# Log-softmax over rows of 50000: dealing a tile's stretches to the partitions in 16 groups of 8

## The chip, the cores and the metric

The kernel runs on one core of one Trainium2 chip. The time is the device time of that core in microseconds (us), the median of several executions. The kernel before takes 7589.62 us (three runs, 7589.4 to 7590.59).

## What is computed

```python
x: (16, 512, 50000) float32, normally distributed

max_x = np.max(x, axis=-1, keepdims=True)
shifted = x - max_x
log_sum_exp = np.log(np.sum(np.exp(shifted), axis=-1, keepdims=True))
return (shifted - log_sum_exp).astype(np.float32)
```

There are 16 x 512 = 8192 rows of 50000 numbers. Input and output are 1638.4 MB each. Every row needs its maximum and the sum of its exponentials before its first output can be written.

## The kernel before

A row is cut into G = 4 parts of 12500 numbers, which is 50000 bytes, and each part lies in one partition. A tile is 32 rows: 128 partitions with one stretch of 50000 bytes each, 6250 KB (of 1024 bytes), and there are 256 tiles. Before the change, partition p of tile t holds stretch p of the tile, so that the four parts of a row are in four neighbouring partitions.

```python
P = 128
SQ = 32          # the transpose works on squares of 32
G = 4            # parts of a row
R = P // G       # rows of a tile
C = 3125         # a piece of a part; NS = 4 pieces
NBUF = 4         # tile buffers
...
xt = xf.rearrange("(t r) (g w) -> t (r g) w", r=R, g=G)
ot = of.rearrange("(t r) (g w) -> t (r g) w", r=R, g=G)

def run(a, first, n):
    part = a[first : first + NBUF * n].rearrange("(q i) p w -> q i p w", i=NBUF)
    return lambda q, i: part[bass.ds(q, 1), i].rearrange("o p w -> (o p) w")
```

The engines run side by side and are joined by semaphores. SyncE issues the loads, one for a tile. The first four are issued at once; each later one waits until the store has emptied its buffer:

```python
def load(j, src):
    sync.dma_start(out=bufs[j], in_=src).then_inc(landed[j], 16)

for t in range(NBUF):
    load(t, xt[t])
src = run(xt, NBUF, rounds)
with sync.Fori(0, rounds) as q:
    for j in range(NBUF):
        take(sync, stored[j])
        load(j, src(q, j))
```

VectorE takes the maximum of each piece (line 197), then the smallest negated maximum of the partition (line 202). In `share` it makes the four partitions of a row agree: a transpose of 32 x 32 squares (line 165), a reduction over the parts of a row (line 168), a copy that gives the result back to each part (line 174), and a transpose back (line 180). It later scales the sums (line 208) and subtracts maximum and logarithm in place (line 185):

```python
vector.transpose(out=allneg, in_=negp.to_broadcast([P, SQ]))
vector.tensor_reduce(
    out=rowneg, in_=allneg.rearrange("p (r g) -> p r g", g=G), op=ALU.min, axis=AX)
vector.tensor_copy(
    out=spread.rearrange("p (r g) -> p r g", g=G),
    in_=rowneg[:, :, None].to_broadcast([P, SQ // G, G]))
vector.transpose(out=negmaxs[k], in_=spread)
...
vector.tensor_scalar(
    out=buf, in0=buf, scalar1=negmaxs[k][:, 0:1], scalar2=logs[k],
    op0=ALU.add, op1=ALU.subtract)
```

(The semaphores are cut from this excerpt.) ScalarE takes the exponentials of each piece and their sum (line 239), and issues the stores. The store of a tile is issued in the middle of the next tile's exponentials; the last tile's goes out in four pieces:

```python
for c in range(NS):
    if c == GATE and dst is not None:
        store((j - 1) % NBUF, dst, bufs[(j - 1) % NBUF])
    ... exponential of piece c of tile j ...
...
for c in range(NS):
    store(NBUF - 1, ot[ntiles - 1][:, cols(c)], bufs[NBUF - 1][:, cols(c)])
```

TensorE adds the sums of a row's parts by a product with a matrix `ones` (line 277), which has a one wherever two partitions hold parts of the same row. GpSimd builds that matrix once, at the start, with a fill and two selections.

Of the kernel before, what the change touches and what calls it, by code (L numbers as in the profile page):

```python
# [10 lines left out]
ALU = mybir.AluOpType  # L11
AX = mybir.AxisListType.X

P = 128
SQ = 32

G = 4
R = P // G
C = 3125
NBUF = 4  # L20

NS = 4

# [21 lines left out]
def take(engine, sem, n=16):  # L45

    engine.wait_ge(sem, n).then_inc(sem, -n)  # L47


def cols(c):  # L50
    return slice(c * C, (c + 1) * C)
# [3 lines left out]
def kernel(  # L55
# [6 lines left out]
    xf = x.flatten_outer_dims()  # L62
    of = out.flatten_outer_dims()
# [3 lines left out]
    ntiles = N // R  # L67


    rounds = (ntiles - NBUF) // NBUF  # L70
    assert ntiles % NBUF == 0 and rounds >= 2

    xt = xf.rearrange("(t r) (g w) -> t (r g) w", r=R, g=G)
    ot = of.rearrange("(t r) (g w) -> t (r g) w", r=R, g=G)

    def run(a, first, n):

        part = a[first : first + NBUF * n].rearrange("(q i) p w -> q i p w", i=NBUF)
        return lambda q, i: part[bass.ds(q, 1), i].rearrange("o p w -> (o p) w")

    data = ctx.enter_context(tc.tile_pool(name="data", bufs=1))
    stats = ctx.enter_context(tc.tile_pool(name="stats", bufs=1))
# [9 lines left out]
    ones = consts.tile([P, P], FP32, name="ones")  # L92
    bufs = [data.tile([P, W], FP32, name=f"buf{j}") for j in range(NBUF)]
    dump = dump_pool.tile([P, C], FP32, name="dump")
    sums = sum_pool.tile([P, NBUF], FP32, name="sums")
    rowsums = [sums[:, k : k + 1] for k in range(NBUF)]

# [15 lines left out]
    def sem(name):  # L113
        return ctx.enter_context(nc.semaphore(name))
# [3 lines left out]
    ready = sem("ones_ready")  # L118
# [11 lines left out]

    @block.gpsimd
    def _(gpsimd):
        view = ones.rearrange("p (r g) -> p r g", g=G)
        gpsimd.memset(ones, 1.0).then_inc(ready)  # L134
        gpsimd.affine_select(  # L135
            out=view, in_=view, pattern=[[-G, R], [0, G]], base=0,
            channel_multiplier=1, compare_op=ALU.is_ge, fill=0.0,
        ).wait_op(ready, 1, "sem-ge").then_inc(ready)
        gpsimd.affine_select(  # L139
            out=view, in_=view, pattern=[[G, R], [0, G]], base=G - 1,  # L140
            channel_multiplier=-1, compare_op=ALU.is_ge, fill=0.0,
        ).wait_op(ready, 2, "sem-ge").then_inc(ready)

    @block.sync
    def _(sync):
# [10 lines that stand above are left out]
        for j in range(NBUF - 1):  # L156
            take(sync, stored[j])
        take(sync, stored[NBUF - 1], 16 * NS)

    @block.vector  # L160
    def _(vector):
        def share(k):

            on_dve.next(
                vector.transpose(out=allneg, in_=negp.to_broadcast([P, SQ]))  # L165
            ).then_inc(on_dve.sem)
            on_dve.next(
                vector.tensor_reduce(  # L168
                    out=rowneg, in_=allneg.rearrange("p (r g) -> p r g", g=G),
                    op=ALU.min, axis=AX,  # L170
                )
            ).then_inc(on_dve.sem)
            on_dve.next(
                vector.tensor_copy(  # L174
                    out=spread.rearrange("p (r g) -> p r g", g=G),
                    in_=rowneg[:, :, None].to_broadcast([P, SQ // G, G]),
                )
            ).then_inc(on_dve.sem)
            on_dve.next(
                vector.transpose(out=negmaxs[k], in_=spread)  # L180
            ).then_inc(agreed.sem)

        def subtract(k, *bufs):
            for n, buf in enumerate(bufs):
                ins = vector.tensor_scalar(  # L185
                    out=buf, in0=buf, scalar1=negmaxs[k][:, 0:1], scalar2=logs[k],
                    op0=ALU.add, op1=ALU.subtract,
                )
                if n == 0:
                    logged.next(ins)  # L190
                ins.then_inc(subtracted.sem)

        def whole(j, by_pieces=False):
            take(vector, landed[j])

            for c in range(NS):
                vector.tensor_reduce(  # L197
                    out=negms[j][:, c : c + 1], in_=bufs[j][:, cols(c)],
                    op=ALU.max, axis=AX, negate=True,
                ).then_inc(shifted.sem if c < NS - 1 else on_dve.sem)  # L200
            on_dve.next(vector.nop()).then_inc(shifted.sem)  # L201
            vector.tensor_reduce(  # L202
                out=negp, in_=negms[j], op=ALU.min, axis=AX
            ).then_inc(on_dve.sem)
            share(j)

            rescaled.next(
                vector.tensor_mul(out=scaleds[j], in0=scales[j], in1=parts[j])  # L208
            ).then_inc(summed.sem)
            subtract(j, *([bufs[j][:, cols(c)] for c in range(NS)] if by_pieces else [bufs[j]]))  # L210

        def settle():
            for count in (on_dve, rescaled, logged):
                count.settle(vector)

        with vector.Fori(0, rounds):
            for j in range(NBUF):
                whole(j)
            settle()
        for j in range(NBUF):  # L220
            whole(j, by_pieces=j == NBUF - 1)

    @block.scalar
    def _(scalar):
        def log(k):
            added.next(
                scalar.activation(out=logs[k], in_=rowsums[k], func=ACT.Ln)  # L227
            ).then_inc(logged.sem)

        def store(j, dst, buf):  # L230
            subtracted.next(scalar.dma_start(out=dst, in_=buf)).then_inc(stored[j], 16)

        def whole(j, dst=None):
# [4 lines that stand above are left out]
                shifted.next(  # L238
                    scalar.activation(  # L239
                        out=dump, in_=bufs[j][:, cols(c)], func=ACT.Exp,  # L240
                        bias=negms[j][:, c : c + 1], scale=1.0,
                        accum_out=parts[j][:, c : c + 1],
                    )
                ).then_inc(on_act.sem)
                on_act.next(scalar.nop())  # L245
            agreed.next(
                scalar.activation(  # L247
                    out=scales[j], in_=negms[j], func=ACT.Exp,
                    bias=negmaxs[j][:, 0:1], scale=-1.0,
                )  # L250
            ).then_inc(rescaled.sem)
            log(j)

        def settle():
            for count in (on_act, shifted, agreed, added, subtracted):
                count.settle(scalar)

        nc.scalar.preload_act_table_set("natural_log_exp_and_others")  # L258
        whole(0)
        settle()  # L260
        dst = run(ot, 0, rounds)
        with scalar.Fori(0, rounds) as q:
            for i in range(NBUF):
                whole((i + 1) % NBUF, dst(q, i))
            settle()
        for t in range(ntiles - NBUF + 1, ntiles - 1):
            whole(t % NBUF, ot[t - 1])
        store(t % NBUF, ot[t], bufs[t % NBUF])
        whole(NBUF - 1)
        for c in range(NS):  # L270
            store(NBUF - 1, ot[ntiles - 1][:, cols(c)], bufs[NBUF - 1][:, cols(c)])

    @block.tensor
    def _(tensor):
        def whole(j):
            for c in range(NS):
                ins = tensor.matmul(  # L277
                    rowsums[j], ones, scaleds[j][:, c : c + 1],
                    start=c == 0, stop=c == NS - 1,
                )  # L280
                if c == 0:
                    summed.next(ins)
            ins.then_inc(added.sem)

        tensor.wait_ge(ready, 3)
        with tensor.Fori(0, rounds):
            for j in range(NBUF):
                whole(j)
            summed.settle(tensor)
        for j in range(NBUF):  # L290
            whole(j)
# [30 lines left out]
```

## Time and profile before

| what | before |
|---|---|
| time, median of 3 | 7589.62 us |
| span of the profiled execution | 7588.4 us |
| VectorE busy | 5440.6 us |
| ScalarE busy | 3184.7 us |
| TensorE busy | 477.9 us |
| bytes moved | 3276.85 MB, mean 432 GB/s |
| a load, from its issue to its landing (median) | 36.7 us |
| a store, likewise | 41.6 us |

A busy time is the time in which an engine had an instruction at work; beside the span it tells how much room the engine has. The transfers run on 16 DMA engines, which loads and stores share; their share of busy time and the GB/s are given for slices of the span. The page also gives, for each queue, the packets and the share of the time of the 16 DMA engines that they took. The trace keeps every packet's start, duration, size and queue, but not the DMA engine that moved it. In the waits, a row names the engine and line that waited, what it waited for, the sum, the number of times and the longest.

### The profile page before, as it was taken

The page shows a single profiled execution, that of the slowest core. Times are in us where ns is not written, and L with a number is a line of the kernel's source. Part 1 is how long each engine was busy: PE and PEld are TensorE (multiplying, and loading weights), DVE is VectorE, ACT ScalarE, POOL GpSimd, SP SyncE. Part 2 cuts the span into 40 slices and gives each one's busy share as a digit, 9 for nine tenths or more (in the row PEclk, how much of TensorE's full clock was granted, in tenths as well). Part 3 has the DMA queues.
Part 4 walks back from the last instruction along what each step waited for, and adds up shares of the span by engine and source line. Part 5 has one row for each costly group of instructions (what it writes and reads, how often), then busy time and mean ns, then how long its engine had stood idle before and what let it go on. Part 6 is the DMA issues. An engine that isn't in the chain of part 4 may idle for free. (4 is left out here: it accounts for less than half of the span.)

```text
span 7588.4 us, 13821 instructions
## 1 busy us (share of the span) xinstructions
PE 477.9 (6%) x2048; PEld 456.0 (6%) x2048; DVE 5440.6 (72%) x2819; ACT 3184.7 (42%) x2561; POOL 1.4 (0%) x7
## 2 busy tenths in 40 slices
PE   0000000000000000000000000000000000000000
PEld 0000000000000000000000000000000000000000
DVE  7767677777777777777777777777777777777776
ACT  4434444344443434444344443434444344444433
POOL 0000000000000000000000000000000000000000
DMA  9999999999999999999999999999999999999999
GB/s 417 432 432 433 434 431 434 434 433 433 434 433 431 434 434 433 431 434 433 432 434 434 431 434 434 432 433 434 434 431 434 434 434 432 434 434 431 434 434 400
DMA packets 74162, 3276.85 MB, mean 432 GB/s; under 512 B 8240, under 2 KB 8240, under 8 KB 8240
## 3 DMA queue, kind: packets, MB, share of 16 engines
q1 hardware_dynamic: 36864, 1638.42, 50.0%
q10 hardware_dynamic: 37296, 1638.42, 50.0%
q14 instruction: 2, 0.02, 0.0%
HBM read 1638.40 MB, written 1638.40 MB: 432 GB/s over the span
## 5 line engine op out<-in xcount | busy, mean ns | idle before, releaser
L239 ACT ACTIVATE dump<-buf,negm 128x3125 f32<-128x3125 f32 x1024 | 2937.3, 2868 | 3805.0 <-DVE negm L197 3765.7
L197 DVE TENSOR_REDUCE negm<-buf 128x1 f32<-128x3125 f32 x1024 | 3418.2, 3400 | 923.3 <-DVEq L47 923.3
L185 DVE TENSOR_SCALAR buf<-buf,negmax,logsum 128x12500 f32<-128x12500 f32 (+1 forms) x259 | 1738.9, 6715 | 553.8 <-ACT logsum L227 553.8
L277 PE MATMUL sums<-scaled,ones 128*128 128x1 f32 x2048 | 477.9, 355 | 7087.2 <-DVE scaled L208 7087.2
L277 PEld LDWEIGHTS sums<-scaled,ones 128*128 128x128 f32 x2048 | 456.0, 328 | 7109.0 <-DVE scaled L208 7109.0
L208 DVE TENSOR_TENSOR scaled<-scale,part 128x4 f32<-128x4 f32 x256 | 41.6, 163 | 580.4 <-ACT scale L247 580.4
L227 ACT ACTIVATE logsum<-sums 128x1 f32<-128x1 f32 x256 | 43.8, 171 | 551.0 <-PE sums L277 551.0
L239 ACT ACTIVATION_READ_ACCUMULATOR dump<-buf,negm 128x1 f32 x1024 | 190.8, 186 | 0.0
L247 ACT ACTIVATE scale<-negm,negmax 128x4 f32<-128x4 f32 x256 | 76.1, 297 | 23.6
L202 DVE TENSOR_REDUCE negp<-negm 128x1 f32<-128x4 f32 x256 | 40.1, 157 | 39.2 <-DVE negm L197 39.2
L180 DVE STREAM_TRANSPOSE negmax<-spread 128x32 f32<-128x32 f32 x256 | 54.2, 212 | 8.9
L165 DVE STREAM_TRANSPOSE allneg<-negp 128x32 f32<-128x32 f32 x256 | 54.1, 211 | 8.9
L168 DVE TENSOR_REDUCE rowneg<-allneg 128x8 f32<-128x32 f32 x256 | 47.6, 186 | 8.9
L174 DVE COPY spread<-rowneg 128x32 f32<-128x32 f32 x256 | 46.3, 181 | 8.9
L258 ACT ACT_TABLE_LOAD x1 | 1.3, 1283 | 1.0 <-SPq L111 1.0
L135 POOL TENSOR_SCALAR_AFFINE_SELECT ones<-ones 128x128 f32<-128x128 f32 x1 | 0.5, 519 | 0.1
L139 POOL TENSOR_SCALAR_AFFINE_SELECT ones<-ones 128x128 f32<-128x128 f32 x1 | 0.5, 519 | 0.1
L134 POOL MEMSET ones<- 128x128 f32 x1 | 0.2, 205 | 0.5 <-SPq L111 0.5
L306 POOL MEMSET const-bfloat16-1.0<- 128x1 bf16 x1 | 0.1, 103 | 0.0
L306 POOL MEMSET const-uint8-127<- 128x1 uint8 x1 | 0.1, 102 | 0.0
L306 POOL MEMSET const-float32-0.0<- 128x1 f32 x1 | 0.1, 99 | 0.3 <-issue 0.3
L306 POOL MEMSET const-float32-1.0<- 128x1 f32 x1 | 0.1, 99 | 0.0
## 6 DMA issues: line engine op xcount, KB each, us to landing
buf<-in_x_dram SPq DMA_DIRECT2D x256, 6250.0 KB, 36.7
out_dram<-buf ACTq DMA_DIRECT2D x255, 6250.0 KB, 41.6
out_dram<-buf ACTq DMA_DIRECT2D x4, 1562.5 KB, 11.3
```

The lines of the kernel that those rows point to most:

```text
L165: vector.transpose(out=allneg, in_=negp.to_broadcast([P, SQ]))
L168: vector.tensor_reduce(out=rowneg, in_=allneg.rearrange("p (r g) -> p r g", g=G), op=ALU.min, axis=AX,)
L174: vector.tensor_copy(out=spread.rearrange("p (r g) -> p r g", g=G), in_=rowneg[:, :, None].to_broadcast([P, SQ // G, G]),)
L180: vector.transpose(out=negmaxs[k], in_=spread)
L185: ins = vector.tensor_scalar(out=buf, in0=buf, scalar1=negmaxs[k][:, 0:1], scalar2=logs[k], op0=ALU.add, op1=ALU.subtract,)
L197: vector.tensor_reduce(out=negms[j][:, c : c + 1], in_=bufs[j][:, cols(c)], op=ALU.max, axis=AX, negate=True,).then_inc(shifted.sem if c < ...
L202: vector.tensor_reduce(out=negp, in_=negms[j], op=ALU.min, axis=AX).then_inc(on_dve.sem)
L208: vector.tensor_mul(out=scaleds[j], in0=scales[j], in1=parts[j])
L227: scalar.activation(out=logs[k], in_=rowsums[k], func=ACT.Ln)
L239: scalar.activation(out=dump, in_=bufs[j][:, cols(c)], func=ACT.Exp, bias=negms[j][:, c : c + 1], scale=1.0, accum_out=parts[j][:, c : c + 1],
L247: scalar.activation(out=scales[j], in_=negms[j], func=ACT.Exp, bias=negmaxs[j][:, 0:1], scale=-1.0,)
L277: ins = tensor.matmul(rowsums[j], ones, scaleds[j][:, c : c + 1], start=c == 0, stop=c == NS - 1,)
```

## The change

The stretches of a tile are dealt to the partitions in another order. Partition p = 8a + b, with a from 0 to 15 and b from 0 to 7, now holds stretch 16b + a of the tile, where before it held stretch p. Sixteen stretches that follow one another in DRAM thus lie in partitions 0, 8, 16, ... 120; the next sixteen lie in partitions 1, 9, 17, and so on. The four parts of a row are 8 partitions apart, and still in one square of 32. [...]

What follows from the new order: the views of a row's parts in `share` step by 8 elements, the matrix `ones` has its ones elsewhere and is built with a fill and four selections, and the last tile's cut stores index one dimension more.

```diff
+STEP = 8
...
-    xt = xf.rearrange("(t r) (g w) -> t (r g) w", r=R, g=G)
-    ot = of.rearrange("(t r) (g w) -> t (r g) w", r=R, g=G)
+    def chunks(a):
+        rows = a.rearrange("n (g w) -> (n g) w", g=G)
+        return rows.rearrange("(t b a) w -> t a b w", a=P // STEP, b=STEP)
+
+    xt, ot = chunks(xf), chunks(of)
...
-        part = a[first : first + NBUF * n].rearrange("(q i) p w -> q i p w", i=NBUF)
-        return lambda q, i: part[bass.ds(q, 1), i].rearrange("o p w -> (o p) w")
+        part = a[first : first + NBUF * n].rearrange("(q i) a b w -> q i a b w", i=NBUF)
+        return lambda q, i: part[bass.ds(q, 1), i].rearrange("o a b w -> (o a) b w")
...
-        gpsimd.memset(ones, 1.0).then_inc(ready)
-        (two selections)
+        view = ones.rearrange("p (b g r) -> p b g r", g=G, r=STEP)
+        gpsimd.memset(ones, 0.0).then_inc(ready)
+        for i in range(G):
+            gpsimd.affine_select(
+                out=view, in_=view, pattern=[[-SQ, P // SQ], [0, G], [-1, STEP]],
+                base=-STEP * i, channel_multiplier=1,
+                compare_op=ALU.not_equal, fill=1.0,
+            ).wait_op(ready, i + 1, "sem-ge").then_inc(ready)
...
-                    out=rowneg, in_=allneg.rearrange("p (r g) -> p r g", g=G),
+                    out=rowneg, in_=allneg.rearrange("p (g r) -> p r g", g=G),
...
-                    out=spread.rearrange("p (r g) -> p r g", g=G),
+                    out=spread.rearrange("p (g r) -> p r g", g=G),
...
-            store(NBUF - 1, ot[ntiles - 1][:, cols(c)], bufs[NBUF - 1][:, cols(c)])
+            store(NBUF - 1, ot[ntiles - 1][:, :, cols(c)], bufs[NBUF - 1][:, cols(c)])
...
-        tensor.wait_ge(ready, 3)
+        tensor.wait_ge(ready, G + 1)
```

More of the change, by code (lines that the diff above doesn't have):

```diff
@@ L132, in _ @@
     def _(gpsimd):
-        view = ones.rearrange("p (r g) -> p r g", g=G)
-        gpsimd.memset(ones, 1.0).then_inc(ready)
[L135 to L142, printed above, removed]
+        view = ones.rearrange("p (b g r) -> p b g r", g=G, r=STEP)
[6 more added lines that the diff above has]
+            ).wait_op(ready, i + 1, "sem-ge").then_inc(ready)
     @block.sync
```

## The prediction

> **What bounds the kernel now.** I read the summary page first (busy shares, then the transfer rows), then the chain that ended last, then the waits, then the table by stage. The first page lines say nearly all of it:
>
> ```profile
> span 7588.4 us, 13821 instructions
> PE 477.9 (6%) x2048; PEld 456.0 (6%) x2048; DVE 5440.6 (72%) x2819; ACT 3184.7 (42%) x2561; POOL 1.4 (0%) x7
> ...
> DMA  9999999999999999999999999999999999999999
> ...
> DMA packets 74162, 3276.85 MB, mean 432 GB/s; under 512 B 8240, under 2 KB 8240, under 8 KB 8240
> ...
> q1 hardware_dynamic: 36864, 1638.42, 50.0%
> q10 hardware_dynamic: 37296, 1638.42, 50.0%
> ```
>
> No compute engine is above 72%. The transfer row is 9 in all forty slices, and the load queue (q1) and the store queue (q10) together took 100.0% of the time of the 16 DMA engines. What is to be seen is that there is no slack in the transfers and that compute has some. The table by stage confirms it (columns: window, length, busy time and count of each engine, clock, DMA share, GB/s):
>
> ```profile
> 0.00:60.00 60.00, 1.87 (x8) 1.78 (x8) 35.46 (x20) 24.41 (x18) 1.45 (x7) 1.00 0.99 413
> 60.00:1000.00 940.00, 59.75 (x256) 57.01 (x256) 679.67 (x352) 397.41 (x321) 0.00 (x0) 1.00 1.00 431
> 1000.00:4000.00 3000.00, 190.43 (x816) 181.69 (x816) 2153.96 (x1114) 1258.23 (x1014) 0.00 (x0) 1.00 1.00 433
> 4000.00:7500.00 3500.00, 220.28 (x944) 210.17 (x944) 2520.45 (x1302) 1476.32 (x1186) 0.00 (x0) 1.00 1.00 433
> ...
> 7550.00:7590.00 40.00, 1.87 (x8) 1.78 (x8) 18.00 (x13) 12.06 (x10) 0.00 (x0) 1.00 0.61 259
> ```
>
> The rate is flat at 431 to 433 GB/s from 60 us on. Only the last 40 us have idle DMA engines: 39% of 40, so 15.6 us, while the last tile is computed and no load is left.
>
> The unit of work is one partition's stretch of 50000 bytes. The load queue has 36864 packets for 256 loads, which is 144 a load, 9 on each of 16 engines: 8 stretches and one small one (the 8240 under 512 bytes are those of 256 + 259 transfers times 16). Half of 16 x 7588.4 us over 256 x 128 = 32768 stretches is 1.85 us each. In the trace's packet records, one by one, a stretch takes 1847 ns at the median, 1846 at the least, and 1851 in the mean. A DMA engine therefore runs at 50000 / 1847 = 27.1 GB/s, and sixteen of them at 433: the rate of the table. One tile is 8 stretches in and 8 out per engine, 16 x 1.85 = 29.6 us, and 256 tiles make 7577 us. That is the kernel.
>
> The waits show the same from the compute side:
>
> ```profile
> DVE negm L197 <- DVEq L47: 923.3, 251, 18.9
> DVE scaled L208 <- ACT scale L247: 580.4, 256, 2.3
> DVE buf L185 <- ACT logsum L227: 553.8, 256, 2.2
> ```
>
> VectorE waits 923.3 us in all (3.7 us a tile) at its line 197 for its own queue, that is for a tile to land. Near the start, where four tiles were loaded ahead, a tile starts every 25.9 us (18.94 to 44.83 in the timeline); near the end every 29.5 (7457.20 to 7486.72). Compute has about 3.6 us of slack a tile.
>
> [...] nothing is in the way now: even in the first 60 us, where all engines load in step, the rate is 413 GB/s.
>
> **The change part by part.**
> 1. Bytes: the same 128 stretches of 50000 bytes each way for a tile, so the same packets. Removed: nothing. On the DRAM side a tile is now 16 x 8 x 12500 elements and not 128 x 12500, in loads and stores. [...]
> 2. Which engine moves what. Before, both sides were cut along a dimension of 128. Now the DRAM side's slowest dimension is 16, and one index of it is 8 neighbouring partitions (p = 8a + b). [...] This is the step that decides, and I can't see it in the trace before.
> 3. What sharing costs. [...] A tile would take 59.2, 44.4 or 29.6 us; 256 of them 15155, 11366 or 7577 us. [...] in the packet records the 16 completions of one load lie 1.1 us apart for the first tiles and 16 us from about tile 36 on.
> 4. What it may bring. [...] All it can remove is what a stretch takes above its floor, 1851 - 1847 = 4 ns, times 4088 stretches an engine (16 a tile, the last tile's store being cut small): 16 us, 0.2%. A smaller spread between engines could save some of the 15.6 us at the end. So at best about 7560 us.
> 5. VectorE: lines 168 and 174 read or write with a step of 8 elements, the same 32 elements per partition, 186 and 181 ns each. Even doubled they add 0.37 us a tile against 3.6 us of slack: nothing at the end, except 0.4 us in the last tile.
> 6. GpSimd: four selections in place of two at 0.52 us add 1.04 us before 4 us, with the first matmul at 36.02: nothing.
>
> **The rivals.** (a) *The transfers stay at their floor*: [...] pairs slip apart until they do not meet. For it: engines drift by 16 us already now[...]. It gives 7560 to 7620 us. (b) *Pairs meet partly*: the start is slow, then leads grow, while some pairs keep meeting; since every tile waits for its slowest pair, one pair is enough. It gives 7750 to 10500. (c) *Pairs stay in step*: the sixteen engines begin their first stretch within 0.9 us, half a stretch, of each other[...]. 11000 to 15000. (d) *DRAM becomes faster or slower by the new order*: bounded by 16 us on the good side; on the bad side nothing in the profile speaks for it[...]. (e) *VectorE becomes the bound*: it would need ten times the cost of step 5.
>
> **Range and chances.** I give (a) 0.39, (b) 0.35, (c) 0.25. A gain of over 2% would need 152 us where at most some 30 exist: 0.01. Weighted with middles of 7590, 8900 and 13000 the mean is about 9300; the middle of the distribution lies lower, as (a) is the largest single lump, and I put the time at 8800. The range reaches from 7560, the best case of step 4, to 13500, which leaves out the worst of (c).
>
> **What would show it.** If step 2 and 3 hold, stretches take well over 1.85 us, up to 3.7, and the first load, 17.8 us to its landing now, takes 25 to 32; the rate of the first 60 us falls from 413 towards 210 to 300 GB/s; the share of DMA time stays near 100% at fewer GB/s; VectorE's wait for landings at its first reduction grows by as much as the span does; and the median landing of 36.7 us for a load grows with the tile. If (a) holds, the packets stay at 1847 ns and all rows of the page but the span's last digits are as before. The prediction is wrong [...] if the pairs part early of themselves; then the time is 7590 within 0.4%.

## The result and the profile after

The changed kernel takes 9997.53 us (median of 4, 9960.76 to 10030.79) where the kernel before takes 7589.74: 1.3171 times as long, 95% interval [1.3136, 1.3205].

The summary page of the changed kernel, the lines that answer to those of before:

```profile
span 9959.0 us, 13826 instructions
PE 478.0 (5%) x2048; PEld 456.1 (5%) x2048; DVE 5450.2 (55%) x2819; ACT 3184.6 (32%) x2561; POOL 2.1 (0%) x9
...
DMA  9999999999999999999999999999999999999999
...
DMA packets 74162, 3276.85 MB, mean 329 GB/s; under 512 B 8240, under 2 KB 8240, under 8 KB 8240
...
q1 hardware_dynamic: 36864, 1638.42, 58.9%
q10 hardware_dynamic: 37296, 1638.42, 41.1%
```

Packets and bytes are the same to the last one, and so are the compute engines' busy times within 10 us. The DMA engines are again busy all the time, but move 329 GB/s and not 432. The two queues no longer share the time evenly: with equal bytes, the loads (q1) now take 58.9% of a longer span, the stores (q10) 41.1%. That is 58.9% x 16 x 9959.0 us over 32768 stretches, 2.86 us a stretch for loads, and 2.0 us for stores, where both took 1.85 before. The packet records agree: means of 2865 and 1997 ns; 8 x (2865 + 1997) ns a tile and 256 tiles give 9957 us, the span. So the whole loss lies in the time of a stretch, and seven eighths of it on the load side (1018 of 1168 ns, taking 1847 ns as the floor of each).

The table by stage (window, length, busy time and count of PE, PEld, DVE, ACT and POOL, clock, DMA share, GB/s):

```profile
0.00:60.00 60.00, 1.87 (x8) 1.78 (x8) 20.14 (x11) 13.72 (x11) 2.06 (x9) 1.00 0.98 204
60.00:1000.00 940.00, 44.82 (x192) 42.76 (x192) 512.04 (x265) 298.44 (x240) 0.00 (x0) 1.00 1.00 323
1000.00:4000.00 3000.00, 145.62 (x624) 138.94 (x624) 1674.76 (x867) 980.02 (x787) 0.00 (x0) 1.00 1.00 336
4000.00:7500.00 3500.00, 169.92 (x728) 162.12 (x728) 1931.19 (x995) 1126.09 (x907) 0.00 (x0) 1.00 1.00 332
```

There are two levels to see. In the first 60 us, with loads alone, the rate is 204 GB/s, half of the 413 before: in the packet records the stretches after an engine's first take 3.65 to 3.93 us, about twice 1.85. Once stores run beside the loads (the first is issued at 75.9 us) it is 323 to 336, and it stays there to the end. The waits show who pays (us in all, times, longest):

```profile
DVE negm L199 <- DVEq L48: 3234.7, 256, 35.2
```

VectorE's wait for a landed tile has grown by 2311 us, of the 2371 us by which the span has grown. A load's median time to landing went from 36.7 to 51.7 us.

### The profile page after: what moved, and what is told of

Its sections match the earlier page's. It is cut to its first block, busy times and chain, and to the rows that moved or that the text cites. A ratio compares the mean times of both kernels' runs of the same rounds, so it can differ in the third digit from the quotient of the medians.

```text
span 9959.0 us, 13826 instructions
## 1 busy us (share of the span) xinstructions
PE 478.0 (5%) x2048; PEld 456.1 (5%) x2048; DVE 5450.2 (55%) x2819; ACT 3184.6 (32%) x2561; POOL 2.1 (0%) x9
## 2 busy tenths in 40 slices
DMA packets 74162, 3276.85 MB, mean 329 GB/s; under 512 B 8240, under 2 KB 8240, under 8 KB 8240
## 3 DMA queue, kind: packets, MB, share of 16 engines
q1 hardware_dynamic: 36864, 1638.42, 58.9%
q10 hardware_dynamic: 37296, 1638.42, 41.1%
## 6 DMA issues: line engine op xcount, KB each, us to landing
buf<-in_x_dram SPq DMA_DIRECT2D x256, 6250.0 KB, 51.7
```

## The experiments

Theory 1: the cut as 16 x 8 changes which DMA engine moves which partitions, and engines then hold each other up in pairs. (The pairs, and that a cut in halves has them and one as 32 x 4 does not, were my estimate: no record names the engine of a packet.) Theory 2: the dealt order in DRAM makes the loads slow. The changed kernel has both at once, so the first runs give each without the other.

| run | DRAM side | order in DRAM | time, us | ratio to before |
|---|---|---|---|---|
| changed kernel | 16 x 8 | dealt | 9997.53 | 1.3171 [1.3136, 1.3205] |
| a_groups4 | 32 x 4 | dealt | 7593.14 | 1.0026 [1.0006, 1.0047] |
| a2_groups4, again | 32 x 4 | dealt | 7593.38 | 1.0015 [1.0004, 1.0027] |
| b_pairs8 | 16 x 8 | pairs of tiles | 9973.58 | 1.3072 [1.304, 1.3104] |
| c_pairs4 | 32 x 4 | pairs of tiles | 7594.19 | 1.0011 [1.0002, 1.0019] |
| d_load_halves | loads 2 x 64 | as before | 9862.07 | 1.2986 [1.2965, 1.3008] |
| e_store_halves | stores 2 x 64 | as before | 9142.04 | 1.2007 [1.1987, 1.2027] |

**a_groups4: dealt, but in groups of 4.**

```diff
-STEP = 8
+STEP = 4
...
-                    out=rowneg, in_=allneg.rearrange("p (g r) -> p r g", g=G),
+                    out=rowneg.rearrange("p (l r) -> p l r", r=STEP),
+                    in_=allneg.rearrange("p (l g r) -> p l r g", g=G, r=STEP),
```

(The copy into `spread` and the matrix `ones` follow in the same way.)

> The changed kernel with 32 groups of 4 partitions in place of 16 groups of 8: partition 4a+b holds stretch 32b+a[...] Theory 1 [...] stretches take 1.85 us in loads and stores, the first 60 us run at about 413 GB/s and the time is 7560 to 7610 us. Theory 2 (the DRAM order is what slows the loads): the order is still dealt, so the time stays near that of the changed kernel, 9500 to 10500 us.

The summary page of this run, queues, and then the first two stages of its table:

```profile
q1 hardware_dynamic: 36864, 1638.42, 50.0%
q10 hardware_dynamic: 37296, 1638.42, 50.0%
```

```profile
0.00:60.00 60.00, 1.86 (x8) 1.78 (x8) 35.53 (x20) 23.63 (x18) 2.73 (x9) 1.00 0.98 413
60.00:1000.00 940.00, 60.79 (x261) 58.05 (x262) 681.04 (x353) 400.27 (x323) 0.00 (x0) 1.00 1.00 431
```

Even queues and 413 GB/s in the first 60 us: the time of before is back, while the order in DRAM is still dealt. That speaks against Theory 2; as this order is not quite the changed kernel's (32b + a in place of 16b + a), the run with loads in halves below, at the addresses of before, decides it. The second, longer series of the same kernel asked whether the order brings anything (it was meant to have stretches that follow one another in DRAM moved at one time; whether it does is in no record):

> The dealt order with 32 groups of 4 again, with more rounds: the first time gave 1.0026 of the kernel before, [1.0006, 1.0047], with single runs up to 7667.87 us. [...] what is left of the difference is the DRAM order and some 34 ns a tile on VectorE: 7588 to 7600 us, a ratio of 0.999 to 1.003. A gain from the DRAM order, the purpose of the change, would show as a ratio under 1.

It does not. Both intervals lie just above 1, so if anything a dealt order costs one to three thousandths. Its single runs scatter more than those of the kernel before: of the 22, fifteen lie between 7590 and 7595 us, six between 7628 and 7752, and one took 7571.54, where the 35 of before lie between 7587 and 7592. In the profiled one, of 7636.32 us, the rate falls from 433 to between 423 and 428 GB/s over the last three eighths of the span, its last 40th aside; the record does not show why.

**b_pairs8 and c_pairs4: another order, cut in both ways.** Two tiles share a stretch of DRAM, in groups of 8 stretches for the first run and of 4 for the second; `ones` and the row parts are those of before.

```diff
-    xt = xf.rearrange("(t r) (g w) -> t (r g) w", r=R, g=G)
+    def chunks(a):
+        rows = a.rearrange("n (g w) -> (n g) w", g=G)
+        return rows.rearrange("(u a h b) w -> u h a b w", a=P // STEP, h=2, b=STEP)
...
```

(The indexing of the tiles follows.)

> The kernel before, with two tiles interleaved in DRAM in groups of 8 stretches: partition 8a+b of a tile holds stretch 16a+b (or 16a+8+b) of the pair, so that a row's parts stay in neighbouring partitions and a group of 8 partitions reads 8 stretches that follow one another, as before; only the DRAM side is now 16 x 8. Theory 1: [...] loads take about 2.9 us a stretch, and the time is 9500 to 10500 us. Theory 2: nothing is dealt in single stretches any more, and the time is 7590 us within 1%.

> The control of the pairs of tiles interleaved in groups of 8: the same kernel with groups of 4, so that the DRAM side is 32 x 4[...]. Nothing else differs in kind: still two tiles interleaved, still the rows' parts in neighbouring partitions. Theory 1 [...]: 1.85 us a stretch, 413 GB/s in the first 60 us, 7580 to 7610 us. If interleaving or a DRAM side of three dimensions cost anything by itself, it would show here: 9000 us or more if that were the whole of the loss of the groups of 8.

The queues of the groups of 8, then those of the groups of 4:

```profile
q1 hardware_dynamic: 36864, 1638.42, 59.2%
q10 hardware_dynamic: 37296, 1638.42, 40.9%
```

```profile
q1 hardware_dynamic: 36864, 1638.42, 50.0%
q10 hardware_dynamic: 37296, 1638.42, 50.0%
```

With groups of 8 the loss is there, in the same proportion of loads to stores, although the eight stretches of a group follow one another in DRAM; with groups of 4 it is gone. So neither the three dimensions of the DRAM side nor the interleaving costs more than two thousandths: the cut decides.

**d_load_halves and e_store_halves: one side alone, at the addresses of before.**

```diff
-            sync.dma_start(out=bufs[j], in_=src).then_inc(landed[j], 16)
+            for h in (slice(0, P // 2), slice(P // 2, P)):
+                sync.dma_start(out=bufs[j][h], in_=src[h]).then_inc(landed[j], 16)
...
```

(The waits count to 32 in place of 16; in the second run the stores are cut in the same way and the loads are whole.)

> The kernel before, with each load issued as two transfers of 64 partitions; the same addresses for every partition, stores untouched. [...] Theory 1: loads are slowed as in the changed kernel, to 2.5 to 3 us a stretch, stores stay at 1.85, so a tile takes 8 x (2.8 + 1.85) = 37 us and the whole 9000 to 9900 us. Theory 2: addresses are unchanged, so 7590 to 7650 us.

> The kernel before, with each store issued as two transfers of 64 partitions, loads untouched. Theory 1, with the difference between loads (2865 ns a stretch in the changed kernel) and stores (1997 ns) [...]: stores take about 2.0 us, a tile 8 x (1.85 + 2.0) = 30.8 us, the whole 7750 to 8000 us. If reads were shared as strictly as writes: 9000 to 9900 us, like the loads in halves. Theory 2: 7590 to 7650 us.

Queues of the run with loads in halves, then of the run with stores in halves:

```profile
q1 hardware_dynamic: 40960, 1638.43, 58.9%
q10 hardware_dynamic: 37296, 1638.42, 40.5%
```

```profile
q10 hardware_dynamic: 41440, 1638.43, 53.2%
q1 hardware_dynamic: 36864, 1638.42, 46.0%
```

The first 60 us of the run with loads in halves:

```profile
0.00:60.00 60.00, 1.86 (x8) 1.78 (x8) 20.43 (x11) 13.72 (x11) 1.45 (x7) 1.00 0.98 202
```

Loads in halves give the changed kernel's picture (half the rate at the start, then mean stretches of 2841 and 1955 ns) without a byte at another address, so Theory 2 falls. Stores in halves missed what I expected by far: 9142 us and not 7750 to 8000. Their stretches take 2390 ns in the mean, and 5036 of 32640 are over 3.65 us. By Theory 1 engines that read from SBUF thus hold each other up as well, and the low mean of the stores in the changed kernel (1997 ns) does not show them free of it. Two more things changed in this run. The loads, which were left as they were, slowed from 1852 to 2066 ns. And of the 1622 us by which the span grew, VectorE's wait for a landed tile took 1166.5; another 428 went to its wait for ScalarE (580.4 to 1008.0 us), which issues the two transfers of each store. That called for transfers alone.

**p1_loads and p2_stores: the changed kernel's transfers, one direction only.** All computation is left out, and in the first nearly all stores, in the second nearly all loads.

```python
# p1_loads                                  # p2_stores
take(sync, landed[j])                       take(scalar, stored[j])
sync.dma_start(out=bufs[j],                 scalar.dma_start(out=dst(q, j),
    in_=src(q, j)).then_inc(landed[j], 16)      in_=bufs[j]).then_inc(stored[j], 16)
```

> Only the 256 loads of the changed kernel (16 groups of 8), four in flight, each issued as soon as its buffer's last load has landed; all computation and all stores but four at the end are left out. Pairs stay in step for good: 256 x 8 stretches of 3.85 us (the start of the changed kernel shows 3.65 to 3.92) are 7900 us, with the four stores some 8000. Pairs slip apart [...]: towards 256 x 8 x 1.85 = 3790 us and 60 for the stores. The DRAM order, were it the cause, would give stretches well over 1.85 us without a ceiling at twice that.

> Only the stores of the changed kernel: four loads at the start, then 256 stores out of the same four buffers, four in flight, nothing computed. [...] stretches of 3.7 to 3.9 us in step and about 8000 us, with a minority near 3.9 us where pairs slip. If reads were nearly free, as the 1997 ns mean of the changed kernel's stores suggested: 2.0 us a stretch and about 4200 us. The stores in halves, with stretches up to 3.9 us, speak for the first.

They took 7985.97 and 4051.89 us, one run each; the kernel before took 7674.81 us in its one run beside these two and the next two. The rate in 40 slices of the span, loads first, then stores:

```profile
GB/s 208 208 208 208 208 208 208 208 208 208 208 208 208 208 208 208 208 208 208 208 208 208 208 208 208 208 208 208 208 208 208 208 208 208 208 208 208 208 208 208
```

```profile
GB/s 205 216 263 331 419 432 433 431 433 433 433 429 433 431 432 431 433 432 431 431 433 431 431 433 432 432 431 434 429 433 431 433 430 432 432 431 431 431 433 324
```

These two lines are the clearest of the study. The loads run at half the rate in every slice: 208 GB/s, a stretch 3847 ns in the mean. In the second line the four loads take the first 127 us, a slice and a quarter. The stores that follow also begin at half the rate, their first sixteen stretches at 3.57 to 3.91 us, but they are at 419 GB/s in the fifth slice of 101 us and at about 432 from then on.

The landing records hold sixteen ends for each transfer (8240 for 515 transfers in the kernel before and in the changed one), which I take as one for each of the 16 DMA engines, and these differ in the same way. Every one of the 256 loads has its sixteen ends within 1.5 us, from the first to the last. The ends of a store lie 1.3 us apart for the first one, 16 us at 280 us, and 37 to 42 us from 450 us on. So with this cut the ends stay together for 8 ms when all transfers write into SBUF, and come apart within a third of a millisecond when all of them read from it. That engines hold each other up in pairs is Theory 1's reading of it. The stores missed the 8000 us that I held likelier; the time is near the 4200 us given for reads that are nearly free, but for another reason: they began at twice the time of a stretch, and then came down to it. The dealt order is the same in both kernels, and at full rate it costs the stores nothing.

**p3_same_half and p4_other_half: do a load and a store of the same partitions slow each other?** Transfers of 64 partitions alone, with the kernel's bytes each way; all computation is left out. The two differ in one word, the half that is stored from (it stands in three places, of which one is shown). If loads and stores of the same partitions slow each other, I expected 10900 us or more of the first, and the second to be faster by 30% or more; if not, the same time for both, about 7570 us where partners take turns.

```diff
-scalar.dma_start(out=dst(q, j), in_=bufs[2 + j][lo]).then_inc(stored[j], 16)
+scalar.dma_start(out=dst(q, j), in_=bufs[2 + j][hi]).then_inc(stored[j], 16)
```

> Transfers alone, as many bytes each way as the kernel has, in pieces of 64 partitions: loads into partitions 0 to 63 of two buffers, stores out of partitions 0 to 63 of two others, nothing computed. [...] An engine moves 2048 stretches in and 2048 out. [...] at best 5.3 us a pair of stretches, 10900 us or more, and no load near 1.85 us beside a store. [...] about 7570 us when the partners alternate, the same as the kernel with stores from the other half.

> As the run with both in the same half, with one difference: stores come out of partitions 64 to 127[...]. Partners that alternate (one loads while the other stores): 1.85 us for most stretches and about 7570 us. Partners in step: 3.9 us for all and up to 16000 us. [...]

10645.29 and 10587.42 us. Queues of the first, then of the second:

```profile
q1 hardware_dynamic: 41120, 1644.83, 61.6%
q10 hardware_dynamic: 40960, 1638.43, 38.4%
```

```profile
q1 hardware_dynamic: 41120, 1644.83, 61.6%
q10 hardware_dynamic: 40960, 1638.43, 38.5%
```

Same shares, and times within 0.6%: whether the stores come out of partitions 0 to 63, into which the loads go, or out of 64 to 127 makes no difference here, so by these two runs, one each, a load and a store of the same partitions do not slow each other. The first time alone would nearly have fitted the 10900 us or more; only the run with the other half decides. By Theory 1, what remains is loads against loads. And the 7570 us of partners that take turns did not come: in the packet records of the second run the middle half of the loads takes 3.0 to 3.4 us a stretch and that of the stores 1.85 to 2.07.

## Why the prediction was right and where it was not

The measured time lies inside the range, and above the 8800 us named. That is in part luck: the range reaches from no loss at all to 13500 us, the largest single chance (0.39) was given to no loss, and 8800 is a balance between three outcomes, of which none had its middle there. What carries weight is the argument, step by step.

- **What bounds the kernel**: right. Every kernel with 16 x 8 or with halves loses in the time of a stretch (its two queues together take 99.2% or more of the DMA engines' time), and VectorE's wait for landings absorbs it, but for the 428 us of stores in halves.
- **Step 2**, the step called deciding: the cut does decide. A cut of 16 x 8 costs 31 to 32%, a cut of 32 x 4 one to three thousandths, and halves at the old addresses 30% for loads and 20% for stores. By what means is not shown: which engine moved which partition is in no record, and that engines meet in pairs was my estimate, which the trace of before could not show. DMA engines without work are not the cause: in the run with loads in halves the mean busy share of the 16 is 0.98 in the first 60 us, at 202 GB/s, where before it is 0.99, at 413. That engines kept clear of each other in groups of 4 is inferred from the time alone (7593.14 and 7594.19 us).
- **Step 3**: the size of a full meeting is right, the working of leads is wrong. Twice the stretch was foretold and 3.65 to 3.93 us came, so that by Theory 1 two engines that meet in their loads carry 208 / 8 = 26.0 GB/s between them, just under the 27.1 of one engine before. But the three times of a tile, 59.2, 44.4 and 29.6 us, were my estimate of twice, one and a half times and once the time of before, as a lead grows, and take a lead to be free once it is long enough. Stores alone behave so: their ends came to lie 37 to 42 us apart, and the rate rose to 432 GB/s. Loads alone never built a lead: 1.5 us at the most. And in the changed kernel the sixteen ends of a load were 7 to 29 us apart after the first millisecond, yet loads took 1.55 times their floor throughout. (That distance is over all sixteen ends; the lead within a pair is not recorded.) It is the mis-sized term: the 8900 us in the middle of the partial case are a factor of 1.17 on the 7577 us of the floor, and loads and stores together took 1.32.
- **Step 4**: the upper bound held, and the gain inside it was nil: 1.0015 and 1.0026 in groups of 4. As stretches took 1847 ns at the median before, and 1851 in the mean, there was nothing for a better order to take away.
- **Steps 5 and 6**: right. The group rows of the changed kernel:

```profile
L170 DVE TENSOR_REDUCE rowneg<-allneg 128x8 f32<-128x32 f32 x256 | 52.8, 206 | 8.9
L176 DVE COPY spread<-rowneg 128x32 f32<-128x32 f32 x256 | 50.0, 195 | 8.9
```

206 and 195 ns where it was 186 and 181: 34 ns a tile, on an engine that now waits 12.6 us for each tile. The four selections are over at 3.1 us.

- **The rivals**: (b) comes nearest. The slow start came (204 GB/s where I gave 210 to 300; the first load landed after 34.1 us where I gave 25 to 32), the ends of a load came apart, and its stretches stayed long, at 2865 ns in the mean. But the partial recovery came with the first stores and not as the ends came apart: from 90 to 160 us the rate was already 317 GB/s, with the ends of a load 5 to 9 us apart, and from 300 to 600 us it was 322, with the ends 21 to 26 us apart. (a), given the largest chance, did not occur: only 9% of the loads' stretches took under 1860 ns, though the ends of a load were up to 29 us apart. (c) is what the loads alone do. (d) and (e) did not occur.

**Open**: why loads alone stay in step while stores alone part; why, with both in flight, stretches end at 2.87 and 2.0 us and not at a clean alternation; and why the side that was left alone slows as well (loads to 2066 ns beside stores in halves, stores to 1955 beside loads in halves, from 1852 and 1850). The records do not name the engine of a packet, nor anything that two engines would share, and I have no run that moves one partner alone.

## What to carry to other kernels

When the DMA engines are the bound, look at how a transfer's DRAM side is cut before its order: here a change of view that left all bytes, packets and issues as they were added 32% to the time. The sign was a share of DMA time at 100% with fewer GB/s (323 to 336 where it was 431 to 433), uneven queues (58.9% and 41.1%), and stretches at up to twice their floor (3.65 to 3.93 us at the start, where it is 1.85). Here a slowest dimension of 128 or 32 gave the full rate (7590 to 7594 us), 16 did not (9997.53 and 9973.58), and neither did two transfers of 64 partitions in place of one of 128 (9862.07 for the loads, 9142.04 for the stores); try the cut on a kernel of loads alone first, where it showed at its plainest: 208 GB/s in every slice.

## What the hardware showed that I had not expected

Cut as 16 x 8, loads alone ran at 208 GB/s for 8 ms, the sixteen ends of a load never more than 1.5 us apart; stores alone began in the same way, at 3.57 to 3.91 us a stretch, had their ends 16 us apart at 280 us and then ran at about 432. Loads and stores of the same partitions did not slow each other: 10645 us, and 10587 with the stores out of the other half, one run each. And in the full kernel stores in halves cost 20%, although stores alone recover (cut as 16 x 8; halves alone were not run); why is not shown.
